# Five row buffers for the gathered expert rows, and another timetable for the dot products around the change of phase

## The chip, the core and the metric

One NeuronCore of a Trainium2 chip runs one program. Its engines are TensorE (PE), VectorE (DVE), ScalarE (ACT), GpSimd (POOL) and SyncE (SP), which issues most of the DMAs; POOL issues the gathers. Each engine works through its own instructions in the order in which they stand in the program, and waits on semaphores where it needs another engine's or a DMA's result. The metric is the time of one execution on the device in microseconds (us), lower is better: the median of three executions.

## The reference

One layer of a hybrid block on 512 tokens of width 1024, in float32. The part that matters here is the second half, a product-key retrieval (PEER) over 128 x 128 = 16384 experts, of which each is one row of `expert_u` and one of `expert_v`:

```python
q = (xb @ w_q).reshape(p, PEER_HEADS, 2, PEER_DK_HALF)
sc = jnp.einsum('phcd,hcnd->phcn', q, sub_keys)
top_s, top_i = lax.top_k(sc, PEER_TOPK)                    # 16 of 128 keys, twice per head
...
best_s, best_pos = lax.top_k(cand_s, PEER_TOPK)            # 16 of the 256 pairs
idx = jnp.take_along_axis(cand_i, best_pos, axis=-1)
g = jax.nn.softmax(best_s, axis=-1)
act = jax.nn.gelu(jnp.einsum('phkd,pd->phk', expert_u[idx], xb), approximate=False)
return jnp.einsum('phk,phkd->pd', g * act, expert_v[idx])  # 8 heads x 16 experts a token
```

Before it stand the adaLN projections, a mixer (gated convolution and RG-LRU) with its projections, and behind it the last residual and RMSNorm.

## The kernel before

**The two ways to the experts.** For 384 of the 512 tokens (tiles 1 to 3) the kernel doesn't gather: it multiplies the tokens with *all* experts and masks with gates. For tile 0, and for the u side of the first 64 tokens of tile 1, it gathers expert rows by index. So the activation phase (u phase) has 128 chunks of 128 experts, and each needs 24 matmuls of 320 columns on PE (`u_chunk`, whose `mm3` splits each product into three of reduced precision: lines 90 to 92), and the value phase (v phase) has 128 chunks of 18 matmuls of 512 columns (`v_chunk`, line 996). Of the 128 u chunks, 124 (`CE`) run in the u phase's loop at line 930, and the last four stand between the first v chunks (list `jobs`).

**What each chunk needs.** SP loads 512 KB of weights (`wraw`, line 71, four buffers, issued up to five chunks ahead and only when a buffer is free). ACT rounds them (`whi`, line 76), DVE makes the rest (`wlo`, line 81, two chunks ahead of PE). In the u phase ACT evicts each chunk's PSUM tile with a GELU (`act`, line 817), and part of the activations is spilled to DRAM (`Ad`). In the v phase every pair of chunks needs the gates (loaded from `Gd` in bursts: lines 847 and 860), `cf` (ACT line 880, DVE line 882), `ch` (ACT line 886) and `cl` (DVE line 893).

**The sparse work.** `dots()` has 192 steps, one for each gathered column of rows: a gather on POOL (`gath`, line 729: 128 rows of 4 KB into a `rows` buffer) and a dot product on DVE (`scr`, line 750). `sums()` has 128 steps: a gather from `v` and a multiply-add on DVE (`ys`, line 766). `ahead()` says how many rows are fetched ahead: the buffer count less one in the u phase, six in the v phase. In the u phase there are `GB_E` = 4 `rows` buffers; late in it three more (`rows2`) come from a pool of the v phase.

**What sets the order.** All of this is one schedule written out by Python. In the u phase, `turn(k)` chooses after each chunk whose generator takes the next step on DVE (searches `s`, remaining searches `r`, gates `g`, dots `d`), as long as the planner's DVE account (`dve[0]`, with 1320 for a dot) is behind its PE account (`pe[0]`, 3530 a chunk). In the v phase a fixed share of the sparse steps follows each chunk (line 1037). At chunk `KD` = 118 the u phase's search and gate work is flushed and its memory is handed to the v phase's pools. `topk_tile` is the search that turns scores into the 16 best experts of a tile, with small SBUF tiles of its own (`cand`, `oh`, `pf`, `bf`, `g`).

In the text chunk k is the u chunk k of the loop at line 930, and v chunk n the n-th chunk of the v phase. On DVE `wlo` of chunk k + 2 stands where the loop is at chunk k.

Of the kernel before, what the change touches and what calls it, by code (L numbers as in the profile page):

```python
# [8 lines left out]
F32 = mybir.dt.float32  # L9
FR = mybir.dt.float32r  # L10
F16 = mybir.dt.float16
# [3 lines left out]
OP = mybir.AluOpType  # L15
# [3 lines left out]
D = 1024  # L19
KB = 8  # L20
NT = 4
NE = 128
# [12 lines left out]
def block_kernel(ctx, tc, xT, small, w_ada1, w_ada, b_ada, w_in, w_r, w_i, w_out, w_q, keys, uT, u, v, final_g, out):  # L35
    nc = tc.nc
# [282 lines left out]
    for cb in range(4):  # L319
# [23 lines left out]
        a = mt("a")  # L343
# [5 lines left out]
        h = mt("h")  # L349
# [67 lines left out]
    sel = ctx.enter_context(tc.tile_pool(name="sel", bufs=1, side="right"))  # L417
# [24 lines left out]
    scp = ep.enter_context(tc.tile_pool(name="scp", bufs=1, side="right"))  # L442
# [63 lines left out]
    topk = ep.enter_context(tc.tile_pool(name="topk", bufs=1))  # L506
# [1 line left out]
    psE = psx.enter_context(tc.tile_pool(name="psE", bufs=1, space=PS))  # L508

    st16 = topk.tile([128, 16], F16, name="st16")  # L510
    s16a = topk.tile([128, 16], F32, name="s16a")
    s16b = topk.tile([128, 16], F32, name="s16b")
    nc.vector.tensor_scalar(s16a, iota[:, :16], 8.0, 8.0, op0=OP.mult, op1=OP.add)
    nc.vector.scalar_tensor_tensor(s16a, iota[:, :16], 16.0, s16a, op0=OP.mult, op1=OP.min)
    nc.vector.tensor_scalar(s16b, iota[:, :16], 4.0, 24.0, op0=OP.mult, op1=OP.add)
# [3 lines left out]
    io16 = topk.tile([128, 16], F16, name="io16")  # L519
# [6 lines left out]
    selB = sel.tile([128, 3, XB], F32, name="selB")  # L526

    def topk_tile(t):
        cand = topk.tile([128, 8, 64], F32, name="cand")
        for a, na, nb, o in ((0, 1, 16, 0), (1, 3, 8, 16), (4, 4, 4, 40), (8, 8, 1, 56)):  # L530
            shc = [128, 8, na, nb]
            nc.vector.tensor_tensor(cand[:, :, o:o + na * nb].rearrange("p h (a b) -> p h a b", b=nb),
# [19 lines left out]
        nc.vector.tensor_tensor(msk, pos, msk, op=OP.bitwise_and)  # L552
        pf = topk.tile([128, 8, 16], F16, name="pf")
        nc.vector.tensor_copy(pf, pos)
        bf = topk.tile([128, 8, 16], F16, name="bf")
        nc.vector.tensor_copy(bf, msk)
        yield 1450
        shp = [128, 8, 16, 16]
        ij = topk.tile([128, 2, 8, 16], F32, name="ij")
        for w in range(2):  # L560
            oh = topk.tile(shp, F16, name="oh")
            yield None
            key, ref, cmp, src = ((pf, st16, OP.is_ge, dif), (bf, io16, OP.is_equal, tif[:, :, 1, :]))[w]
            nc.scalar.activation(oh, key[:, :, :, None].to_broadcast(shp), AF.Copy)
            ac[0] += 1930
            if w == 0:
                nc.scalar.activation(g, g, AF.Exp)
            yield None
            nc.vector.tensor_tensor(oh, oh, ref[:, None, None, :].to_broadcast(shp), op=cmp)
            nc.vector.tensor_tensor(oh, oh, src[:, :, None, :].to_broadcast(shp), op=OP.mult)  # L570
            yield 2300
            for n in (8, 4, 2):
                nc.vector.tensor_add(oh[:, :, :, 0:n], oh[:, :, :, 0:n], oh[:, :, :, n:2 * n])
            nc.vector.tensor_add(ij[:, w], oh[:, :, :, 0], oh[:, :, :, 1])
            yield 1400
# [111 lines left out]
    def gates_E():  # L687
        for t in range(1, NT):
            while gready.get(t, NE) > cur[0]:
                yield None  # L690
            yield from gates_tile(t, range(4 if t == 1 else 0, 8), selT[t])
        while len(bdone) < XB:
            yield None
        yield None
        for e in range(2):
            es = slice(XB * e, XB * (e + 1))
            nc.scalar.activation(act_p[es, es], act_b[es, :], AF.Gelu)
        pt = psE.tile([128, 4, 128], F32, name="ps_t")
        nc.tensor.matmul(pt[:, 0, 0:XB], act_p, sel2, start=True, stop=True)
        yield None  # L700
        nc.vector.tensor_mul(selB[:, 2, :], pt[:, 0, 0:XB], selB[:, 2, :])
        yield from gates_tile(1, range(4), selB, 0)
        while gpre or gpost or stores:
            gates_step(None)
            yield None

    acts = sel.tile([128, 128], F32, name="acts")
    act_b = sel.tile([128, XB], F32, name="act_b")
    act_p = sel.tile([128, 2 * XB], F32, name="act_p")
    nc.vector.memset(act_p, 0.0)  # L710
    bdone = []

    rows = {}
    late = []
    taken = [0]

    def row_tile():
        taken[0] += 1
        if late and taken[0] > late[1] and taken[0] % 7 in (1, 3, 5):
            return late[0].tile([128, D], F32, name="rows2", bufs=3)  # L720
        return rowp.tile([128, D], F32, name="rows", bufs=GB_E)

    def ahead():
# [181 lines left out]
    def turn(k):  # L905

        awake = [g for g in "gsrd" if g in gens and asleep[g] <= k]
        if gopen and "g" in gens:
            gt = 96 * (k + 1 - gopen[0]) / (KD - KG - gopen[0])
            if "g" in awake and given["g"] < gt and ac[0] < pe[0] + AD:  # L910
                return "g"
            if "s" in awake and (given["g"] < gt and ac[0] < pe[0] + AD or given["s"] < NS * (k - gopen[0]) / (KD - gopen[0])):
                return "s"
        elif "s" in awake:
            return "s"
        elif "r" in awake and ("d" not in awake or given["d"] >= DS * (k - first[0])):
            return "r"
        for g in "dsg" if ac[0] < pe[0] + AD else "ds":
            if g in awake:
                return g  # L920
# [92 lines left out]
    for k in range(CE, len(jobs)):  # L1013
# [20 lines left out]
            pe[0] += 4090  # L1034
            dve[0] += 2005
        if kind == "v":
            share = min((n + 1) / (NE - VE), 1) * (steps + 0.31 * (NE - RB)) - 0.31 * max(n + 1 - RB, 0)
            while done < share and next(sparse, None):
                done += 1
    fin = vp.tile([128, 2, 3, D], F32, name="gt", bufs=1)  # L1040
# [40 lines left out]
XB = 64  # L1081
# [9 lines left out]
DS = 1.0  # L1091
XD = 1
CE = 124
GB_E = 4
RB = 32
ZL = 1
XE = 5
# [52 lines left out]
```

## Time and profile before

| | |
|---|---|
| Median of three executions | 1411.56 us (1410.68 to 1412.37) |
| The profiled execution | 1409.24 us |
| Its span from the first instruction to the last | 1407.5 us |
| PE / DVE / ACT / POOL busy | 96% / 87% / 52% / 38% of the span |
| First u chunk on PE | 310 us from the span's start |
| Last matmul of the u phase's loop | 839.5 us |
| Last matmul | 1393 us |
| DMA | 440.10 MB, mean 313 GB/s |

Times in views of the trace are us from the span's start. An engine's busy time is the union of its instructions' times; PE's instructions overlap each other, so that its busy share says little, and the distance from one matmul's start to the next is what counts. In a row of the timeline stand start, duration, engine, line, operation, what is written and read; in square brackets the idle time of the engine before it, and who ended it. A `DMA share` of about 1 says that all 16 DMA engines were occupied.

### The profile page before, as it was taken

What the parts mean: (1) busy time and instruction counts of PE and PEld (TensorE: products, weight loads), DVE (VectorE), ACT (ScalarE), POOL (GpSimd) and SP (SyncE); (2) the same over time, 40 slices, a digit from 0 to 9 for tenths busy, and PEclk for the clock granted to TensorE, in tenths of its full rate; (3) what the DMA queues carried; (4) which work ended last, traced back from release to release, by engine and by line L of the source; (5) the groups of instructions that cost most, each with busy time, mean ns of one, the idle gap of its engine ahead of it and who ended that gap; (6) DMA issues with size and microseconds to landing.
All of it is one profiled execution on the core that took longest, in us unless ns stands there. A gap on an engine that the chain in (4) does not pass through costs nothing.

```text
span 1407.5 us, 22023 instructions
## 1 busy us (share of the span) xinstructions
PE 1357.2 (96%) x7739; PEld 1176.0 (84%) x7739; DVE 1231.5 (87%) x2470; ACT 735.2 (52%) x1212; POOL 540.1 (38%) x334
## 2 busy tenths in 40 slices
PE   5999998999999999999999989999999999999996
PEld 2566777779999999999999988877778888878884
DVE  6676565799999999989999967989989898999998
ACT  3554433536489699956996533333333333343342
POOL 0000000000135434514333335666757676766770
PEclk9999999999999999999999999999999999999998
DMA  9575323124689899978999899999999999999994
GB/s 378 213 256 197 132 85 103 53 91 138 206 273 406 320 346 367 391 251 309 353 369 373 301 402 383 368 359 413 410 413 414 415 412 415 414 407 413 414 369 177
DMA packets 146931, 440.10 MB, mean 313 GB/s; under 512 B 14722, under 2 KB 42370, under 8 KB 144772
## 3 DMA queue, kind: packets, MB, share of 16 engines
q1 hardware_dynamic: 99812, 267.75, 51.4%
q0 software_dynamic: 46720, 169.89, 31.5%
q8 instruction: 61, 1.00, 0.3%
q10 hardware_dynamic: 288, 1.05, 0.2%
q14 instruction: 50, 0.41, 0.1%
HBM read 393.54 MB, written 45.09 MB: 312 GB/s over the span
## 4 chain that ended last, share of the span: by engine, by line
PE 32%; issue 24%; DMA 20%; DVE 16%; POOL 6%; ACT 1%; DVEq 0%; POOLq 0%; SPq 0%; ACTq 0%
DMA wraw<-in_v_dram 13%; PE acc L996 7%; POOL rows L729 6%; PE ps_z L90 5%; PE ps_z L92 5%; PE ps_z L91 5%; DMA rows<-in_u_dram,idx_s 3%; DVE wlo L81 3%; DVE scr L750 3%; DVE ys L766 3%; DMA rows<-in_u_dram,idx_b 2%; PE ps_act L90 2%; DVE cf L882 2%; PE ps_act L91 2%; PE ps_act L92 2%
## 5 line engine op out<-in xcount | busy, mean ns | idle before, releaser
L76 ACT ACTIVATE whi<-wraw 128x1024 fp32r<-128x1024 f32 x292 | 308.4, 1057 | 392.9 <-DMA wraw<-in_v_dram 170.0
L81 DVE TENSOR_TENSOR wlo<-wraw,whi 128x1024 fp32r<-128x1024 f32 x292 | 356.1, 1221 | 82.5 <-ACT whi L76 81.3
L90 PE MATMUL ps_act<-h,whi 128*128 128x320 f32 x1024 | 322.4, 315 | 1.5 <-ACT sc L494 1.2
L91 PE MATMUL ps_act<-h,whi 128*128 128x320 f32 x1024 | 317.0, 310 | 0.0
L92 PE MATMUL ps_act<-h,wlo 128*128 128x320 f32 x1024 | 316.8, 309 | 0.0
L729 POOL DMA_INDIRECT rows<-in_u_dram,idx_s x128 | 201.1, 1571 | 226.5 <-DVE scr L750 187.3
L729 POOL DMA_INDIRECT rows<-in_v_dram,idx_s x128 | 234.7, 1833 | 108.9 <-DVE ys L766 82.1
L996 PE MATMUL acc<-whi,cl 128*128 128x512 f32 x750 | 232.7, 392 | 6.1 <-DVE cl L893 6.1
L996 PE MATMUL acc<-whi,ch 128*128 128x512 f32 x750 | 232.8, 391 | 5.2 <-ACT act L817 3.9
L996 PE MATMUL acc<-wlo,ch 128*128 128x512 f32 x750 | 232.0, 390 | 0.0
L90 PEld LDWEIGHTS ps_act<-h,whi 128*128 128x128 f32 x1024 | 193.0, 189 | 2.1 <-ACT sc L494 1.4
L91 PEld LDWEIGHTS ps_act<-h,whi 128*128 128x128 f32 x1024 | 193.0, 189 | 0.2
L92 PEld LDWEIGHTS ps_act<-h,wlo 128*128 128x128 f32 x1024 | 192.7, 188 | 0.0
L729 POOL DMA_INDIRECT rows<-in_u_dram,idx_b x64 | 99.2, 1550 | 211.7 <-DVE scr L750 105.6
L996 PEld LDWEIGHTS acc<-whi,cl 128*128 128x128 f32 x750 | 140.5, 189 | 38.8 <-DVE cl L893 10.2
L996 PEld LDWEIGHTS acc<-whi,ch 128*128 128x128 f32 x750 | 141.0, 188 | 35.7 <-ACT act L817 4.7
L996 PEld LDWEIGHTS acc<-wlo,ch 128*128 128x128 f32 x750 | 141.4, 189 | 29.7
L766 DVE SCALAR_TENSOR_TENSOR ys<-rows,acts,ys 128x1024 f32<-128x1024 f32 x127 | 162.8, 1282 | 1.6
L750 DVE SCALAR_TENSOR_TENSOR scr<-rows,h2n 128x1024 f16<-128x1024 f32 x128 | 156.4, 1222 | 8.2 <-DMA rows<-in_u_dram,idx_s 6.7
L406 POOL DMA_DIRECT2D x1d<-xn x8 | 4.6, 569 | 282.5 <-DVE wlo L81 234.9
L817 ACT ACTIVATE act<-ps_act 128x320 f32<-128x320 f32 x128 | 55.4, 433 | 102.3 <-PE ps_act L92 100.4
L621 PE MATMUL ps_gt<-igh,jh 128*128 128x128 f32 x768 | 97.4, 275 | 2.6 <-DVE igh L615 0.9
(258 smaller groups left out, 1888.4 us busy)
## 6 DMA issues: line engine op xcount, KB each, us to landing
wraw<-in_uT_dram SPq DMA_DIRECT2D x128, 512.0 KB, 6.8
wraw<-in_v_dram SPq DMA_DIRECT2D x128, 512.0 KB, 10.1
Gd<-stg SPq DMA_DIRECT2D x46, 512.0 KB, 7.0
wada<-in_w_ada_dram SPq DMA_DIRECT2D x16, 1024.0 KB, 5.3
Ad<-act SPq DMA_DIRECT2D x48, 320.0 KB, 7.7
act<-Ad SPq DMA_DIRECT2D x48, 320.0 KB, 11.4
h<-Gd SPq DMA_DIRECT2D x12, 1024.0 KB, 17.7
wraw<-in_w_in_dram SPq DMA_DIRECT2D x20, 512.0 KB, 6.0
```

The costliest lines, as they stand in the source:

```text
L76: nc.scalar.activation(hi, raw, AF.Copy)
L81: nc.vector.tensor_sub(lo, raw, hi.bitcast(F32))
L90: nc.tensor.matmul(ps, hi[:, k, :], xh(k), start=first and k == ks[0], stop=False)
L91: nc.tensor.matmul(ps, hi[:, k, :], xl(k), start=False, stop=False)
L92: nc.tensor.matmul(ps, lo[:, k, :], xh(k), start=False, stop=last and k == ks[-1])
L621: nc.tensor.matmul(pg[:, :, k], jh[:, k, :], ig[:, k, :], start=True, stop=True)
L729: nc.gpsimd.indirect_dma_start(out=r[:, :], out_offset=None, in_=table, in_offset=bass.IndirectOffsetOnAxis(ap=idxs[:, k:k + 1], axis=0))
L750: nc.vector.scalar_tensor_tensor(scr, rows.pop(n), 1.0, hn, op0=OP.mult, op1=OP.mult, accum_out=dst[:, k:k + 1])
L766: nc.vector.scalar_tensor_tensor(ys, rows.pop(k), acts[:, k:k + 1], ys, op0=OP.mult, op1=OP.add)
L817: nc.scalar.activation(act[c // 2][:, c % 2], ps, AF.Gelu)
L882: nc.vector.tensor_mul(cf[:, :, XB:].rearrange("p c (g t) -> p c g t", t=16), act.pop(vorder[2 * q] // 2).rearrange("p c (g t) -> p c g t" ...
L996: nc.tensor.matmul(accs[b][e], st[:, bs], mv[:, e * 512:(e + 1) * 512], start=first, stop=last)
```

## The change

**Memory, and with it a fifth row buffer.** Some small tiles lose their own memory: `cand` now lies in the `oh` buffer, the second key (`bf`) takes the `pf` buffer after the first has been read, `act_p` takes the `g` buffer, and the two constants `s16a` and `s16b` two `rep` buffers. `GB_E` goes from 4 to 5, so that the u phase fetches four rows ahead; of the late `rows2` there are two in place of three, so that the v phase still has seven.

**The dots' timetable.** `turn` leaves the dots out of the choice when more than `DR` = 1.15 dots a chunk were given so far, from chunk `CE - QU` = 118 on, and when the chunk has had one (even chunks) or two (odd chunks); before, a chunk's dots were limited (to `XD` = 1) only once the gates' generator had ended. In the v phase the sparse steps begin `QV` = 3 chunks later, and the line of line 1037 is steeper so that it ends where it did.

```diff
-    s16a = topk.tile([128, 16], F32, name="s16a")
-    s16b = topk.tile([128, 16], F32, name="s16b")
+    s16a, s16b = (scp.tile([128, 128], F32, name="rep", bufs=2)[:, 0:16] for _ in range(2))
...
-        cand = topk.tile([128, 8, 64], F32, name="cand")
+        cand = topk.tile([128, 8, 16, 16], F16, name="oh").rearrange("p h a b -> p (h a b)").bitcast(F32)
+        cand = cand[:, 0:512].rearrange("p (h c) -> p h c", h=8)
...
-        bf = topk.tile([128, 8, 16], F16, name="bf")
-        nc.vector.tensor_copy(bf, msk)
-        yield 1450
+        yield 1350
...
             oh = topk.tile(shp, F16, name="oh")
+            if w == 1:
+                pf = topk.tile([128, 8, 16], F16, name="pf")
+                nc.vector.tensor_copy(pf, msk)
             yield None
-            key, ref, cmp, src = ((pf, st16, OP.is_ge, dif), (bf, io16, OP.is_equal, tif[:, :, 1, :]))[w]
+            key, ref, cmp, src = ((pf, st16, OP.is_ge, dif), (pf, io16, OP.is_equal, tif[:, :, 1, :]))[w]
...
+        act_p = topk.tile([128, 8, 16], F32, name="g").rearrange("p a b -> p (a b)")
+        nc.vector.memset(act_p, 0.0)
         for e in range(2):
...
-    act_p = sel.tile([128, 2 * XB], F32, name="act_p")
-    nc.vector.memset(act_p, 0.0)
...
-        if late and taken[0] > late[1] and taken[0] % 7 in (1, 3, 5):
-            return late[0].tile([128, D], F32, name="rows2", bufs=3)
+        if late and taken[0] > late[1] and taken[0] % 7 in (2, 5):
+            return late[0].tile([128, D], F32, name="rows2", bufs=2)
...
         awake = [g for g in "gsrd" if g in gens and asleep[g] <= k]
+        if "d" in awake and (given["d"] >= DR * (k + 1 - first[0]) or k >= CE - QU or xd > k % 2):
+            awake.remove("d")
...
-            share = min((n + 1) / (NE - VE), 1) * (steps + 0.31 * (NE - RB)) - 0.31 * max(n + 1 - RB, 0)
+            share = min(max(n + 1 - QV, 0) / (NE - VE - QV), 1) * (steps + 0.31 * (NE - RB)) - 0.31 * max(n + 1 - RB, 0)
...
-GB_E = 4
+GB_E = 5
+DR = 1.15
+QU = 6
+QV = 3
```

**What moves on DVE at the change of phase.** This is DVE's order in the kernel before, from the `wlo` that stands at loop chunk 117 to the first `cf` of the v phase; each L750 row is a dot product.

```order
L81 TENSOR_TENSOR wlo<-wraw,whi 128x1024
L750 SCALAR_TENSOR_TENSOR scr,acts<-rows,h2n 128x1024
L81 TENSOR_TENSOR wlo<-wraw,whi 128x1024 x2
L750 SCALAR_TENSOR_TENSOR scr,acts<-rows,h2n 128x1024
L81 TENSOR_TENSOR wlo<-wraw,whi 128x1024
L750 SCALAR_TENSOR_TENSOR scr,acts<-rows,h2n 128x1024
L81 TENSOR_TENSOR wlo<-wraw,whi 128x1024
L750 SCALAR_TENSOR_TENSOR scr,acts<-rows,h2n 128x1024
L81 TENSOR_TENSOR wlo<-wraw,whi 128x1024
L750 SCALAR_TENSOR_TENSOR scr,acts<-rows,h2n 128x1024
L882 TENSOR_TENSOR cf<-act,gt 128x2x320
```

The same place in the changed kernel, where a dot product has line 751 and `cf` and `cl` have lines 883 and 894; it goes on to the first dots of the v phase.

```order
L81 TENSOR_TENSOR wlo<-wraw,whi 128x1024
L751 SCALAR_TENSOR_TENSOR scr,acts<-rows,h2n 128x1024
L81 TENSOR_TENSOR wlo<-wraw,whi 128x1024 x5
L883 TENSOR_TENSOR cf<-act,gt 128x2x320
L81 TENSOR_TENSOR wlo<-wraw,whi 128x1024
L894 TENSOR_TENSOR cl<-cf,ch 128x768
L81 TENSOR_TENSOR wlo<-wraw,whi 128x1024
L883 TENSOR_TENSOR cf<-act,gt 128x2x320
L81 TENSOR_TENSOR wlo<-wraw,whi 128x1024 x2
L894 TENSOR_TENSOR cl<-cf,ch 128x768
L81 TENSOR_TENSOR wlo<-wraw,whi 128x1024 x2
L883 TENSOR_TENSOR cf<-act,gt 128x2x320
```

The dots after loop chunk 117 are gone from here, and with them the gathers that their buffers would have released on POOL; the next dot stands behind v chunk 3. Counted through the whole order: up to chunk 117 both kernels have 111 of the 192 dots; in chunks 118 to 123 the kernel before has 5 and the changed one none; behind them stand 76 before and 81 now.

**What moves on DVE in the v phase.** The kernel before at v chunks 12 and 13, with the `cf` of one pair of chunks and its `cl`:

```order
L81 TENSOR_TENSOR wlo<-wraw,whi 128x1024
L882 TENSOR_TENSOR cf<-act,gt 128x2x320
L750 SCALAR_TENSOR_TENSOR scr,acts<-rows,h2n 128x1024
L81 TENSOR_TENSOR wlo<-wraw,whi 128x1024
L893 TENSOR_TENSOR cl<-cf,ch 128x768
L750 SCALAR_TENSOR_TENSOR scr,acts<-rows_10028,h2n 128x1024
L750 SCALAR_TENSOR_TENSOR scr,acts<-rows,h2n 128x1024
```

The changed kernel at the same two chunks (`rows_10012` is a buffer of the `rows2` pool):

```order
L81 TENSOR_TENSOR wlo<-wraw,whi 128x1024
L883 TENSOR_TENSOR cf<-act,gt 128x2x320
L751 SCALAR_TENSOR_TENSOR scr,acts<-rows,h2n 128x1024
L751 SCALAR_TENSOR_TENSOR scr,acts<-rows_10012,h2n 128x1024
L81 TENSOR_TENSOR wlo<-wraw,whi 128x1024
L894 TENSOR_TENSOR cl<-cf,ch 128x768
L751 SCALAR_TENSOR_TENSOR scr,acts<-rows,h2n 128x1024 x2
```

Where the kernel before now and then has one dot a chunk, the changed one has two nearly throughout. By the line of line 1037, with 76 + 128 = 204 and 81 + 128 = 209 steps, a chunk had (204 + 29.76) / 127 = 1.84 steps up to v chunk 31 and 0.31 fewer behind it, 1.53; now it has none in three chunks, then (209 + 29.76) / 124 = 1.93, and behind v chunk 31 1.62.

## Prediction

> **What bounds the kernel now.** I read the page's busy shares and slices first, then busy time by stretches, then the waits of PE, then the timeline around each wait.
>
> ```profile
> PE 1357.2 (96%) x7739; PEld 1176.0 (84%) x7739; DVE 1231.5 (87%) x2470; ACT 735.2 (52%) x1212; POOL 540.1 (38%) x334
> DVE  6676565799999999989999967989989898999998
> ```
>
> PE's 96% says little, since its matmuls overlap; the slices say that from the eighth on DVE is nearly as full as PE. So the question is who waits for whom. These are the waits of PE in four stretches: the u phase (320 to 839 us), the change of phase (839 to 880), the first v chunks with dots (880 to 1048), and the rest of the v phase (1048 to 1382).
>
> ```profile
> PE ps_gt L621 <- DVE igh L615: 0.9, 2, 0.6
> PE acc L996 <- ACT act L817: 3.9, 2, 3.5
> PE acc L996 <- DVE cl L893: 5.3, 7, 2.2
> PE acc L996 <- ACT ch L886: 1.3, 2, 0.9
> PE acc L996 <- DVE cl L893: 0.8, 1, 0.8
> ```
>
> The first row, the longest of the u phase, is under a microsecond in 519: PE paces the u phase. At the change of phase PE waits 3.9 us in two waits, in the first dot-laden v chunks 6.6 us, and in the last 334 us once. All that a new timetable can win lies in these places.
>
> The largest is the change of phase. PE's last u matmul, its first two v matmuls, and the first matmul behind the first v chunk:
>
> ```profile
> 839.45 0.31 PE L92 MATMUL ps_act<-h,wlo 128*128 128x320 f32 x1
> 843.22 0.80 PE L996 MATMUL acc<-whi,ch 128*128 128x512 f32 x1 [3.46 <-ACT act L817]
> 844.49 0.80 PE L996 MATMUL acc<-whi,ch 128*128 128x512 f32 x1 [0.48 <-ACT act L817]
> 850.60 0.31 PE L90 MATMUL ps_act<-h,whi 128*128 128x320 f32 x1
> 842.00:849.00 7.00, 5.30 (x12) 3.87 (x13) 6.96 (x9) 2.44 (x4) 2.09 (x2) 0.51 1.06 340
> 1100.00:1200.00 100.00, 100.00 (x442) 82.68 (x442) 94.10 (x88) 40.23 (x51) 68.15 (x37) 1.00 1.03 414
> ```
>
> The last two rows are stretches; their columns are the stretch, its length, busy time (and instructions) of PE, PE's weight loads, DVE, ACT and POOL, the granted clock, DMA share and GB/s. An undisturbed v chunk costs 18 x 100/442 = 4.07 us. From 839.60 (one u step of 0.15 behind the last) to 850.60 pass 11.0 us: **6.9 us are lost here**, 3.6 before the first matmul and 3.3 after it, about one of those at the second wait and the rest because PE's clock stood at 0.51 after the gap.
>
> Why PE waits there is on ACT, DVE and SP:
>
> ```profile
> 840.71 1.06 ACT L76 ACTIVATE whi<-wraw 128x1024 fp32r<-128x1024 f32 x1 [7.52 <-DMA wraw<-in_uT_dram]
> 842.75 0.42 ACT L817 ACTIVATE act<-ps_act 128x320 f32<-128x320 f32 x1
> 844.02 0.42 ACT L817 ACTIVATE act<-ps_act 128x320 f32<-128x320 f32 x1
> 838.62 0.82 DVE L882 TENSOR_TENSOR cf<-act,gt 128x640 f32<-128x640 f32 x1 [4.90 <-DMA gt<-Gd]
> 823.22 6.81 SPq L860 DMA_DIRECT2D gt<-Gd  x3
> 830.08 3.70 SPq L71 DMA_DIRECT2D wraw<-in_uT_dram  x1
> ```
>
> ACT is in order, and the rounding of u chunk 124's weights holds up everything behind it for 7.5 us: the `ch` of v chunk 0 and the two evictions. Those weights were issued only at 830, behind three gate loads that took SP 6.8 us to issue, and landed 10.6 us later. The DMA engines were full (this stretch, with POOL's column showing who shares them):
>
> ```profile
> 800.00:830.00 30.00, 30.00 (x211) 30.00 (x210) 24.68 (x36) 12.29 (x18) 16.60 (x12) 1.00 1.03 408
> 830.00:870.00 40.00, 36.07 (x196) 32.52 (x195) 25.86 (x32) 14.89 (x21) 15.30 (x12) 0.91 1.02 380
> ```
>
> POOL's 12 instructions are gathers of 128 x 4 KB = 0.524 MB: 6.3 of the 12.2 MB of 800 to 830.
>
> **The change part by part.** *The empty chunks around the change of phase.* Five dots and their gathers leave chunks 118 to 123, and none come back before v chunk 3 (some 862 us by the old clock). From about 820 to 862 the gathers, half of the traffic above, are gone. Then the gates land several microseconds before 838, and the weights issued at 830 or sooner take less than their 10.6 us. Late next is the eviction of the last u chunk, which can't start before that chunk's matmuls end (839.76) and takes 0.42 us, so the second v matmul starts near 840.3 in place of 839.8. I leave 0.6 us of the 6.9, and no halved clock behind so short a gap. **Term: -6.3 us**, bounds -6.9 (nothing left) and 0 (below, the rival in which SP is the cause).
>
> *First v chunks.* These rows are DVE's dots and weight splits from 930 to 1003, and the stretch itself:
>
> ```profile
> L750 DVE SCALAR_TENSOR_TENSOR scr<-rows,h2n 128x1024 f16<-128x1024 f32 x32 | 39.1, 1222 | 0.5
> 930.00:1003.00 73.00, 69.93 (x301) 55.60 (x300) 69.49 (x97) 25.51 (x33) 52.07 (x31) 1.00 1.02 400
> ```
>
> DVE works 69.5 of 73 us, so here it sets the pace, and PE waits for `cl`. From v chunk 17 to 31 the new line has 1.93 - 1.84 = 0.09 more dots a chunk: 15 x 0.09 x 1.22 = 1.6 us, and none of it is covered. The three chunks without dots don't help, because `wlo` can't run further ahead than its buffers. **Term: +1.6 us** (bounds 0, if the lead that DVE brings from there covers it, and 4: all 31 - 3 chunks at that rate, 3.1, and a longer wait at the first load of gates).
>
> *Rest of the v phase.* DVE's three large groups from 1048 to 1382, the waits of ACT for weights in the v phase, and PE's wait behind such a late load (the first, in the stretch above):
>
> ```profile
> L766 DVE SCALAR_TENSOR_TENSOR ys<-rows,acts,ys 128x1024 f32<-128x1024 f32 x126 | 161.5, 1282 | 1.6
> L81 DVE TENSOR_TENSOR wlo<-wraw,whi 128x1024 fp32r<-128x1024 f32 x83 | 101.2, 1220 | 16.6 <-ACT whi L76 16.6
> ACT whi L76 <- DMA wraw<-in_v_dram: 169.4, 63, 8.0
> 929.19 0.74 PE L996 MATMUL acc<-whi,cl 128*128 128x512 f32 x2 [2.17 <-DVE cl L893]
> ```
>
> DVE is idle 16.6 + 1.6 = 18.2 us here, nearly all waiting for weights. The new line adds 1.62 - 1.53 = 0.09 steps in each of 81 chunks: 7.3 x 1.28 = 9.3 us of DVE work, half of that idle time. On average it fits; but the idle time comes when loads are late, once in 16 chunks with the gates, and then DVE's work is not ahead as far as it was: 16 x 0.09 x 1.28 = 1.8 us a burst. PE has room there except where it waits already, which is at two of the five bursts behind chunk 31 (one in the row of 5.3 us, one the 0.8). I charge these two with 0.8 each. **Term: +1.6 us** (bounds 0 and 5 x 1.8 = 9.2).
>
> *The u phase.* The number of dots up to chunk 117 is the same (111); they are only spread more evenly, and a fifth buffer fetches a row more ahead. DVE's waits for rows late in the u phase, from 800 to 842:
>
> ```profile
> DVE scr L750 <- DMA rows<-in_u_dram,idx_s: 4.8, 5, 1.5
> ```
>
> These 4.8 us go, and cost PE nothing before (no wait of PE names DVE there beyond the 0.9 above). Sharing buffers costs no new wait of weight: `cand`, `oh` and `pf` are written and read in turn by DVE in order, and ACT's copy into `oh` waited for DVE's `pf` before as well. If DVE's work comes too late for a gate matmul, PE waits as in that 0.9 row. **Term: 0**, bounds -0.9 (that wait gone) and +1.8 (twice as much on top). The moved constants and the later `memset` are under 1 us of DVE work each beside chunks that PE paces: nothing.
>
> *Sum.* -6.3 + 1.6 + 1.6 + 0 = -3.1 us. The profiled execution took 1409.24 us (span 1407.5 and 1.7 around it), so it becomes 1406.1; the median of the runs lies 2.3 us above that execution, and the forecast for the median is 1411.56 - 3.1 = **1408.5 us**.
>
> **The rivals.** *Nothing is given back.* The added DVE work hides: for it, the one wait of PE after 1048; against it, the DVE-paced stretch before. Then 1411.56 - 6.3 = 1405.3 us.
>
> *The stall stays, because SP and not the gathers makes it.* SP took 6.8 us to issue three gate loads, and the weights behind them came late for that reason; if issuing is what takes the time, taking gathers away moves little. [...] Against it, two rows of the same trace, a larger gate load later on, and its size:
>
> ```profile
> 892.51 0.44 SPq L847 DMA_DIRECT2D h<-Gd  x1
> h<-Gd SPq DMA_DIRECT2D x12, 1024.0 KB, 17.7
> gt<-Gd SPq DMA_DIRECT2D x6, 512.0 KB, 10.2
> ```
>
> A load of 1024 KB is issued in 0.44 us, three of 512 KB in 6.8: so SP was held up by full engines, and this rival is the less likely. It gives 1411.56 + 3.2 = 1414.8 us, or less with half of the stall gone.
>
> *The DMA engines become the bound of the v phase, and it ends slower.* The place is v chunk 3 to about 110. Before that point the old kernel had already issued gathers that the new one has still to issue: ten between 843 and 869 (the 12 of the row 830 to 870, less two before 843), and four in balance before 843 (76 + 128 steps less three rows ahead, against 81 + 128 less four). That is 14 x 0.524 = 7.3 MB, and at 412 GB/s, which the trace reaches (row 1100 to 1200: 414), 17.8 us. Old stretches with room take some of it:
>
> ```profile
> 870.00:900.00 30.00, 30.00 (x142) 25.41 (x142) 27.81 (x41) 11.83 (x17) 19.52 (x12) 1.00 0.96 358
> 900.00:1000.00 100.00, 94.77 (x410) 75.88 (x409) 89.63 (x123) 35.80 (x46) 65.58 (x41) 1.00 1.01 394
> ```
>
> 54 x 30 + 18 x 100 GB/s us = 3.4 MB, 8.3 us. The rest, 9.5 us, would be PE's wait: 1411.56 - 6.3 + 9.5 = 1414.8 us. It decides from the point where rows are read as soon as they land; before, `ys` waited 1.6 us in 126 times, so rows come early, and the lead can shrink instead. [...] The page's slices of GB/s never show more than 415:
>
> ```profile
> GB/s 378 213 256 197 132 85 103 53 91 138 206 273 406 320 346 367 391 251 309 353 369 373 301 402 383 368 359 413 410 413 414 415 412 415 414 407 413 414 369 177
> ```
>
> So I keep the 412.
>
> **How the numbers follow.** The forecast (with its own range 1406 to 1411) has 0.45, nothing given back 0.25, the stall that stays 0.12, DMA as the bound 0.13, anything else 0.05. About 0.2%, 2.8 us, is what a measurement of this kernel can tell from no change. Faster than 1408.7 are the second case and half of the first, 0.48; slower than 1414.4 the last two in part and most of the rest, 0.17; between them 0.35. The range leaves out a tenth on each side: below, a clean gain of more than 7; above, the bounds of the v terms: 1404 to 1415.
>
> **What would show it.** Right: the gap between the last u matmul and the first v matmul under 1 us, clock 1.00 there, no POOL gather from some 820 us to v chunk 3, PE's waits for `cl` from v chunk 17 to 31 longer by one to two us, waits after 1048 two or three in place of one. Wrong: a gap above 2 us with SP still several us in the gate loads (the second rival), or DVE waiting for `rows` in the v phase (the third), or PE waits of several us before chunk 118 for gates.

## The result, and the profile after

| | before | after |
|---|---|---|
| Median of six executions | 1410.74 us (1408.89 to 1412.37) | 1420.61 us (1418.6 to 1423.04) |
| The profiled execution, its span | 1409.24, 1407.5 us | 1418.6, 1416.8 us |

The changed kernel is slower: the ratio is 1.0074, with a 95% interval from 1.0063 to 1.0085. The forecast was 1408.5 us and its range ended at 1415.

From the page of the changed kernel, the busy shares, DVE's slices and the slices of GB/s (a slice is 35.4 us):

```profile
PE 1357.7 (96%) x7739; PEld 1175.0 (83%) x7739; DVE 1233.2 (87%) x2472; ACT 733.5 (52%) x1208; POOL 518.1 (37%) x334
DVE  6676555899999999899999947799999899899998
GB/s 378 208 267 193 121 89 97 60 83 149 219 304 391 293 355 370 339 254 344 373 365 349 386 352 219 408 377 415 411 416 412 414 412 413 407 415 411 399 382 171
```

The busy shares are those of before. What stands out are two slices. The 25th, from 850 to 885 us, moved 219 GB/s where the kernel before moved 383; the one ahead of it 352 where that moved 402. Over the same stretch DVE drops to 4 and 7 tenths.

**The change of phase** went as the prediction said. PE's last u matmul, its first two v matmuls and the first matmul behind the first v chunk stand in the timeline of PE; the weights of u chunk 124 in that of ACT; the gate loads in that of SP:

```profile
839.15 0.31 PE L92 MATMUL ps_act<-h,wlo 128*128 128x320 f32 x1
839.29 0.40 PE L999 MATMUL acc<-whi,ch 128*128 128x512 f32 x1
839.98 0.50 PE L999 MATMUL acc<-whi,ch 128*128 128x512 f32 x1 [0.29 <-ACT act L818]
834.61 1.06 ACT L76 ACTIVATE whi<-wraw 128x1024 fp32r<-128x1024 f32 x1 [1.72 <-DMA wraw<-in_uT_dram]
818.20 9.07 SPq L861 DMA_DIRECT2D gt<-Gd  x3
```

The v phase begins directly behind the u phase, and the matmul behind the first v chunk starts at 843.97. By the prediction's own measure (from the last u matmul on, less 0.15 and 4.07 us) 0.60 us are lost here, where the kernel before lost 6.93: **6.3 us gained**, exactly the term. SP still takes 9.07 us in the gate loads; from 818 to 828 us the DMA share was 1.05, at 399 GB/s.

**Where the time came from instead.** The last u matmul stands 0.3 us earlier than before and 6.3 us were gained behind it, but the span is 9.3 us longer. So the rest of the program lost 9.3 + 6.3 + 0.3 = 15.9 us. PE's waits in the changed kernel, first from 880 to 1048 us, then from 1048 to 1395:

```profile
PE acc L999 <- ACT ch L887: 5.8, 2, 3.7
PE acc L999 <- DVE cl L894: 2.7, 4, 1.4
PE acc L999 <- DVE cl L894: 3.8, 5, 2.4
PE acc L999 <- ACT ch L887: 2.3, 2, 1.7
PE acc L992 <- DVE cl L894: 1.6, 1, 1.6
```

They are 8.5 us in place of 6.6, and 7.7 in place of 0.8: 8.8 us more. In the first stretch it is the waits that name `ch` that grew, from 1.3 to 5.8; those for `cl` fell from 5.3 to 2.7. And three times the granted clock fell, in stretches of 4 us (columns as in the prediction, the clock third from the end):

```profile
915.00:919.00 4.00, 4.00 (x11) 3.10 (x12) 3.37 (x6) 0.09 (x1) 1.59 (x1) 0.58 1.06 407
980.00:984.00 4.00, 4.00 (x11) 2.93 (x11) 3.93 (x7) 1.06 (x1) 2.04 (x2) 0.57 1.03 419
1110.00:1114.00 4.00, 4.00 (x13) 3.12 (x12) 3.96 (x5) 2.10 (x3) 2.17 (x2) 0.57 1.03 418
```

I estimate the cost of each from its clock, 4 x 0.43 = 1.7 us, so 5.1 together. Waits and clock make 13.9 of the 15.9 us; where the other two go isn't shown.

**What PE waits for.** The longest wait, in ACT's and PE's timeline:

```profile
912.81 1.06 ACT L76 ACTIVATE whi<-wraw 128x1024 fp32r<-128x1024 f32 x1 [12.62 <-DMA wraw<-in_v_dram]
914.99 0.73 PE L999 MATMUL acc<-whi,ch 128*128 128x512 f32 x2 [3.66 <-ACT ch L887]
```

PE names ACT, and ACT had waited 12.6 us for a load of weights, with `ch` queued behind it. Over the later v phase (1048 to 1395) ACT's waits for weights are, before and after:

```profile
ACT whi L76 <- DMA wraw<-in_v_dram: 102.4, 41, 8.0
```

```profile
ACT whi L76 <- DMA wraw<-in_v_dram: 126.2, 50, 7.7
```

DVE, on which the prediction priced this phase, is not fuller. These are its groups from 1048 to 1382 us, and its only wait for rows from 880 on:

```profile
L767 DVE SCALAR_TENSOR_TENSOR ys<-rows,acts,ys 128x1024 f32<-128x1024 f32 x122 | 156.3, 1281 | 1.6
L81 DVE TENSOR_TENSOR wlo<-wraw,whi 128x1024 fp32r<-128x1024 f32 x80 | 97.6, 1221 | 18.6 <-ACT whi L76 18.6
DVE scr L751 <- DMA rows<-in_u_dram,idx_s: 0.4, 1, 0.4
```

It sits idle 1.6 + 18.6 us, as it did before (1.6 + 16.6). What was given up is DMA time. The stretches of the changed kernel:

```profile
820.00:862.00 42.00, 41.71 (x255) 39.21 (x254) 18.80 (x18) 17.47 (x25) 0.00 (x0) 1.00 0.82 284
862.00:880.00 18.00, 18.00 (x92) 15.62 (x91) 15.89 (x23) 7.20 (x10) 9.64 (x6) 1.00 0.72 245
880.00:1000.00 120.00, 112.31 (x475) 90.41 (x474) 108.44 (x151) 40.99 (x53) 80.34 (x51) 0.97 1.01 397
1000.00:1100.00 100.00, 99.16 (x438) 81.80 (x437) 92.28 (x113) 35.72 (x46) 62.70 (x39) 1.00 1.04 413
```

and of the kernel before:

```profile
820.00:862.00 42.00, 38.07 (x221) 35.30 (x220) 29.30 (x37) 14.29 (x22) 15.35 (x12) 0.92 1.03 384
862.00:880.00 18.00, 18.00 (x98) 16.06 (x97) 13.81 (x19) 8.15 (x12) 9.90 (x7) 1.00 0.99 392
880.00:1000.00 120.00, 114.77 (x498) 92.45 (x497) 109.49 (x152) 43.35 (x56) 80.57 (x49) 1.00 1.00 385
1000.00:1100.00 100.00, 98.64 (x434) 81.03 (x433) 91.57 (x105) 35.87 (x47) 64.13 (x39) 1.00 1.03 412
```

From 820 to 880 the changed kernel moves 284 x 42 + 245 x 18 = 16.3 MB, the kernel before 23.2: 6.85 MB are left for later, 16.6 us at 412 GB/s. The bytes are the same in all (440.10 MB), and from 1000 us on both kernels run at 412 to 413 with the DMA share above 1, although the changed one has 5.4 MB more waiting: there is nothing to catch up with. Only 880 to 1000 took something, (397 - 385) x 120 = 1.4 MB or 3.5 us. POOL shows what is missing:

```profile
816.06 0.94 POOL L730 DMA_INDIRECT rows<-in_u_dram,idx_s  x1 [3.10 <-DVE scr L751]
864.01 1.80 POOL L730 DMA_INDIRECT rows<-in_u_dram,idx_s  x1 [47.01 <-DVE scr L751]
```

No gather starts for 48 us, because all five buffers are full and the next dot that frees one stands behind v chunk 3. At 864 the first one goes; 6 gathers start from 820 to 880, where the kernel before has 19.

### The profile page after: what moved, and what is told of

Its sections match the earlier page's. It is cut to its first block, busy times and chain, and to the rows that moved or that the text cites. A ratio compares the mean times of both kernels' runs of the same rounds, so it can differ in the third digit from the quotient of the medians.

```text
span 1416.8 us, 22009 instructions
## 1 busy us (share of the span) xinstructions
PE 1357.7 (96%) x7739; PEld 1175.0 (83%) x7739; DVE 1233.2 (87%) x2472; ACT 733.5 (52%) x1208; POOL 518.1 (37%) x334
## 2 busy tenths in 40 slices
DMA packets 146931, 440.10 MB, mean 311 GB/s; under 512 B 14722, under 2 KB 42370, under 8 KB 144772
## 3 DMA queue, kind: packets, MB, share of 16 engines
q10 hardware_dynamic: 288, 1.05, 0.2%
## 4 chain that ended last, share of the span: by engine, by line
issue 26%; DVE 26%; PE 24%; DMA 15%; POOL 6%; ACT 2%; DVEq 0%; POOLq 0%; SPq 0%; ACTq 0%
DMA wraw<-in_v_dram 12%; POOL rows L730 6%; DVE wlo L81 5%; PE ps_z L90 4%; PE ps_z L92 4%; PE ps_z L91 4%; DVE ys L767 4%; DVE scr L751 3%; DVE cf L883 2%; DVE cl L894 2%; PE acc L999 2%; PE ps_act L90 2%; PE ps_act L92 2%; PE ps_act L91 2%; PE ps_gt L622 2%
## 5 line engine op out<-in xcount | busy, mean ns | idle before, releaser
L730 POOL DMA_INDIRECT rows<-in_v_dram,idx_s x128 | 218.8, 1709 | 113.2 <-DVE ys L767 90.3
L730 POOL DMA_INDIRECT rows<-in_u_dram,idx_b x64 | 91.9, 1436 | 249.9 <-DVE scr L751 128.0
```

Of the source, the lines that this page charges most:

```text
L730: nc.gpsimd.indirect_dma_start(out=r[:, :], out_offset=None, in_=table, in_offset=bass.IndirectOffsetOnAxis(ap=idxs[:, k:k + 1], axis=0))
```

## The experiments

Three theories were put against each other. **A**: the gathers left out of the emptied chunks come back where the DMA engines are full. **B**: the fifth buffer, the split of the late buffers and the shared tiles cost it. **C**: DVE has more steps a chunk in the v phase. All runs stand beside executions of the kernel before on the same chip (medians 1409.5 to 1410.2). "Lost" is the change of phase measured as above, "MB" what the DMA moved from 820 to 880 us, and "gathers" how many started there. "Behind" is the rest of the profiled execution, from the first matmul behind the first v chunk to the end of the span; "lost" and "behind" are of one execution each, the median is of several.

| Kernel | gathers | MB | lost, us | behind, us | median, us | ratio to before |
|---|---|---|---|---|---|---|
| before | 19 | 23.2 | 6.9 | 556.9 | 1410.7 | |
| after | 6 | 16.3 | 0.6 | 572.8 | 1420.6 | 1.0074 [1.0063, 1.0085] |
| e1 both stretches filled | 18 | 20.9 | 1.6 | 560.7 | 1404.8 | 0.9967 [0.9957, 0.9978] |
| e2 emptied stretches alone | 8 | 17.6 | 1.8 | 578.4 | 1424.1 | 1.0094 [1.0077, 1.0111] |
| e3 14 gathers left out | 6 | 16.5 | 0.6 | 563.6 | 1410.2 | 1.0008 [0.9998, 1.0018] |
| e4 14 dots made short | 6 | 16.6 | 0.6 | 573.4 | 1419.7 | 1.0068 [1.0051, 1.0085] |
| e5 end of the u phase empty | 13 | 19.3 | 0.6 | 568.2 | 1412.8 | 1.0022 [1.0013, 1.0031] |
| e6 start of the v phase empty | 11 | 18.4 | 2.7 | 570.4 | 1417.0 | 1.0048 [1.0035, 1.0062] |
| e7 five buffers alone | 17 | 22.2 | 7.6 | 555.8 | 1408.5 | 0.9987 [0.9975, 1.0] |
| e8 even dots alone | 19 | 22.4 | 4.3 | 557.8 | 1404.6 | 0.9962 [0.9948, 0.9975] |
| e9 gathers early | 8 | 17.1 | 0.6 | 569.7 | 1417.0 | 1.0052 [1.0037, 1.0067] |
| e10 seven buffers at once | 16 | 21.7 | 6.9 | 557.7 | 1409.7 | 1.0004 [0.9992, 1.0015] |
| e11 gate loads apart | 17 | 22.0 | 4.4 | 554.3 | 1405.5 | 0.9969 [0.9958, 0.998] |
| e12 v dots sooner | 20 | 23.2 | 2.6 | 557.1 | 1405.7 | 0.9972 [0.9963, 0.9982] |

### Which part does the harm: e1 and e2

e1 is the changed kernel with both stretches filled again; e2 is the kernel before with nothing but the two stretches.

```diff
-QU = 6
-QV = 3
+QU = 0
+QV = 0
```

> The changed kernel without the two edits that empty the chunks around the change of phase (the cut-off from chunk 118 on and the three v chunks without sparse steps): five buffers, shared tiles and the even spread of the dots stay, and the dots stand in the same numbers as in the kernel before (111 up to chunk 117, 5 in chunks 118 to 123, 6 in the first three v chunks). Theory A (DMA: the gathers that leave the emptied chunks come back where the DMA engines are full) gives the time of the kernel before, 1409 to 1412 us, with PE's wait of some 4 us back at the change of phase. Theory B (the fifth buffer with its 5 + 2 split, or the shared tiles, cost the time) gives 1417 to 1421.

```diff
         awake = [g for g in "gsrd" if g in gens and asleep[g] <= k]
+        if "d" in awake and k >= CE - QU:
+            awake.remove("d")
...
-            share = min((n + 1) / (NE - VE), 1) * (steps + 0.31 * (NE - RB)) - 0.31 * max(n + 1 - RB, 0)
+            share = min(max(n + 1 - QV, 0) / (NE - VE - QV), 1) * (steps + 0.31 * (NE - RB)) - 0.31 * max(n + 1 - RB, 0)
```

> The kernel before, four buffers, with those two edits alone. Theory A gives 1418 to 1422 us, theory B 1404 to 1411. Both expect PE's wait at the change of phase to be under 1 us.

e1 took 1404.8 us, 15.8 less than the changed kernel and less than the kernel before; e2 took 1424.1. So the emptied stretches do the harm, and without the rest of the change they do no less (1424.1 lies above A's range too, but the intervals of e2 and of the changed kernel overlap); theory B falls. e1 came out below what A expected too, because the wait at the change of phase hardly returned. In e1, PE's wait there and the stretches:

```profile
PE acc L999 <- ACT act L818: 1.3, 1, 1.3
820.00:862.00 42.00, 40.73 (x248) 38.18 (x247) 26.06 (x33) 15.16 (x22) 11.38 (x9) 1.00 0.95 339
862.00:880.00 18.00, 18.00 (x94) 15.77 (x93) 17.86 (x26) 8.31 (x12) 13.93 (x10) 1.00 0.98 371
```

It loses 1.6 us there although the dots stay in chunks 118 to 123. This loss isn't the same in each execution: e6, e11 and e12, whose program is that of e1 up to this place, lose 2.7, 4.4 and 2.6 in theirs. Emptying the chunks bought one to four microseconds on top of that, and cost all the rest.

### Gathers or dots: e3 and e4

In e3 fourteen of the gathers behind the emptied stretch are left out (those dots read `h2n` in their place); in e4 the gathers stay and the same fourteen dots cover 64 of 1024 columns.

```diff
+        if table is u and key in SKIP:
+            rows.setdefault(key, h2n)
...
+SKIP = range(131, 187, 4)
```

> The changed kernel without the gathers of 14 of its 128 u rows for tile 0, every fourth from row column 67 on (v chunks 14 to 44); their dot products stay and read another tile instead, so that 14 columns of these activations are not the reference's. DVE's work is the same. Theory A: 14 x 0.524 MB at 412 GB/s are 17.8 us of DMA time less, and most of what the change lost comes back: 1405 to 1411 us. Theory C (DVE: more sparse steps a chunk are what PE waits for) expects 1418 to 1421.

```diff
-            nc.vector.scalar_tensor_tensor(scr, rows.pop(n), 1.0, hn, op0=OP.mult, op1=OP.mult,
+            w = 64 if n in SKIP else D
+            nc.vector.scalar_tensor_tensor(scr[:, 0:w], rows.pop(n)[:, 0:w], 1.0, hn[:, 0:w], op0=OP.mult, op1=OP.mult,
...
+SKIP = range(131, 187, 4)
```

> The changed kernel with the gathers of those same 14 columns, but their dot products over 64 of the 1024 columns of a row, so that these 14 columns of activations are not the reference's. DMA's work is the same, DVE's is 14 x 1.1 = 15 us less. Theory C expects 1405 to 1412 us, theory A 1417 to 1421.

Without the gathers the time falls by 10.4 us; with the dots cut short, by 0.9, which lies within the spread of the changed kernel's executions, though DVE is busy for 14.9 us less from 880 to 1380 us (449.0 in place of 464.0). Theory C falls. The 10.4 us are 0.74 a gather, less than its 0.524 MB at 412 GB/s (1.27 us). My guess, which no run tests, is that the debt was paid off slowly, since only one dot in four lost its gather; the first long wait, at 912 us, stayed (3.9 us; 3.7 in the changed kernel).

### Which of the two stretches: e5 and e6

The changed kernel with `QV = 0` (e5) and with `QU = 0` (e6).

> The changed kernel with QV = 0: the chunks 118 to 123 stay without dots, the first v chunks get theirs back (dots up to chunk 117, in 118 to 123, in v chunks 0 to 2, in 3 to 15, in 16 to 31, later: 111, 0, 6, 25, 30, 20). Beside the kernel with both stretches filled (1404.8) five dots and their gathers are moved out, beside the changed kernel (1420.6) six are moved back. If every moved gather costs its share of the 15.8 us between those two (1.4 us each): 1411 to 1413, with DMA at 820 to 862 below 320 GB/s and at 862 to 880 above 340. If the v chunks' gap alone does the harm: 1404 to 1406. If the gap at the end of the u phase alone does it: 1419 to 1421.

> The changed kernel with QU = 0: dots in chunks 118 to 123 stay, the v phase begins with three chunks without (111, 5, 0, 25, 30, 21). Six dots and their gathers are moved out. By 1.4 us each: 1412 to 1415, with DMA at 862 to 880 below 300 GB/s. If the gap at the end of the u phase alone does the harm: 1404 to 1406; if that of the v chunks alone: 1419 to 1421. In all cases the wait at the change of phase should be about that of the kernel with both filled (1.3 us), not of the kernel before (6.9).

1412.8 and 1417.0 us: 8.0 and 12.2 above e1, so both stretches cost. Together they cost 15.8, less than the sum. The 1.4 us a dot of the expectation held for the five of e5 (1.6) and was low for the six of e6 (2.0). The stretch from 862 to 880 us, first in e5, then in e6:

```profile
862.00:880.00 18.00, 18.00 (x89) 15.49 (x89) 15.89 (x22) 7.94 (x11) 10.51 (x7) 1.00 0.77 267
```

```profile
862.00:880.00 18.00, 18.00 (x96) 15.92 (x95) 15.58 (x21) 6.24 (x9) 8.21 (x6) 1.00 0.66 227
```

For e5 the expectation was wrong here (above 340), and from 820 to 862 us too (344 GB/s, below 320 expected). The late buffers count from the tenth gather behind chunk 118 on, so with five dots fewer the fill-up to seven buffers, at 868 to 877 us in e1, comes at 879 to 886: the missing dots leave the next stretch emptier too.

### What makes e1 faster than the kernel before: e7 and e8

e7 is the changed kernel without its timetable (`QU = 0`, `QV = 0`, and the two lines in `turn` left out); e8 is the kernel before with the rule on the number of dots and nothing else:

```diff
         awake = [g for g in "gsrd" if g in gens and asleep[g] <= k]
+        if "d" in awake and (given["d"] >= DR * (k + 1 - first[0]) or xd > k % 2):
+            awake.remove("d")
...
 GB_E = 4
+DR = 1.15
```

> The changed kernel without any of the new timetable (QU = 0, QV = 0, and the line in turn that drops the dots left out): five row buffers and the shared tiles alone, dots 112, 5, 6, 24, 29, 16. If the fifth buffer makes the gain of the kernel with both stretches filled (it lets a gather start before the burst of weight and gate loads): 1404 to 1406, and a wait of 1 to 2 us at the change of phase. If spreading the dots (DR and the limit a chunk) makes it: 1409 to 1411 as before, and about 7 us lost at the change of phase.

> The kernel before with the line in turn that holds the dots to DR = 1.15 a chunk and to one or two in a chunk, and with nothing else: four row buffers, no stretch without dots (112, 5, 6, 24, 29, 16). The mirror of the run before: if spreading makes the gain, 1404 to 1406 with the wait at the change of phase at 1 to 2 us; if the fifth buffer makes it, 1409 to 1411 with about 7 us lost there. If it needs both, both runs stay at 1408 to 1411.

(The numbers of dots in the expectation of e8 are those of e7; e8 has 111, 5, 6, 24, 29, 17.) Five buffers alone give 1408.5 us, and the loss at the change of phase stays, 7.6 us. The rule alone gives 1404.6, with four buffers, and the loss goes down to 4.3, not to the 1 to 2 us of the expectation. The profiled execution of e8 is 3.4 us shorter than that of the kernel before: 2.7 less is lost at the change of phase, the last u matmul stands 1.7 earlier, and behind there are 0.9 more. What the rule moves is small: the kernel before and e7 have 12 dots in chunks 110 to 117, e8 and e1 have 10. It shows in the arrival of u chunk 124's weights, ACT's rows of e7, e1 and e10 (below):

```profile
841.04 1.06 ACT L76 ACTIVATE whi<-wraw 128x1024 fp32r<-128x1024 f32 x1 [8.21 <-DMA wraw<-in_uT_dram]
```

```profile
836.41 1.06 ACT L76 ACTIVATE whi<-wraw 128x1024 fp32r<-128x1024 f32 x1 [3.53 <-DMA wraw<-in_uT_dram]
```

```profile
841.45 1.06 ACT L76 ACTIVATE whi<-wraw 128x1024 fp32r<-128x1024 f32 x1 [7.81 <-DMA wraw<-in_uT_dram]
```

From 799 to 838 us the kernel before, e7 and e10 start 13 gathers each, and the weights come at 840.7, 841.0 and 841.5; e1, e2, e6, e8, e11 and e12 start 9 to 11, and they come between 836.1 and 838.7; the changed kernel starts 7, and they come at 834.6. The losses go with them: 6.9 to 7.6 us, 1.6 to 4.4, and 0.6. So the stall goes with the last few gathers ahead of the change of phase. With two to four of the thirteen away, between two fifths (e11) and five sixths (e1) of the 6.3 us are gained that taking six away gains.

### Moving gathers alone: e9 and e10

In both the two late buffers count from chunk 118 on; e9 is otherwise the changed kernel and issues a gather after each of four chunks, e10 is e1. DVE's order is kept.

```diff
-            late[:] = [gp, taken[0] + 10]
+            late[:] = [gp, taken[0]]
+        if KD < k < KD + 5:
+            pre = len(bdone) + k - KD + 2
+            gath(u, usteps[pre][0], usteps[pre][3], pre)
```

> The changed kernel, in which only gathers are moved: the two late row buffers count from chunk 118 on, and one gather each is issued in chunks 119 to 122, so that five rows and not three lie ready when the dots begin again behind v chunk 3, and the fill-up to seven buffers at 893 us falls into the empty stretch. DVE's order, with its stretch of nine chunks without dots, stays. If the DMA engines' work left out of that stretch is what costs (15.8 us for the twelve gathers that the kernel with both stretches filled has issued more by 880 us), four gathers earlier are worth 3 to 5 us: 1415 to 1418, with more than 284 GB/s at 820 to 862. If the dots' place on DVE costs: 1419 to 1422. If it is only the burst of gathers at 893 beside the gate loads: the wait of 3.66 us at 915 is gone and the time falls by 4, with the later waits for cl and ch unchanged.

> The kernel with QU = 0 and QV = 0 (1404.8), with the two late row buffers counted from chunk 118 on in place of ten gathers later, so that the two gathers of the fill-up come at 820 to 850 us (339 GB/s there, about 3 MB of room) and not at 868 to 877. If DMA work done before 880 us is worth its time at 412 GB/s: 2 gathers, 1.05 MB, up to 2.5 us less, 1402 to 1404. If that stretch is too close to the change of phase and its gate loads: the wait there (1.3 us) grows by as much, 1404 to 1406.

e9 took 1417.0 us, 3.6 less than the changed kernel and within A's range, but not as meant. Only one gather came early:

```profile
824.98 1.04 POOL L730 DMA_INDIRECT rows<-in_u_dram,idx_s  x1 [7.31 <-DMA Ad<-act]
864.68 1.80 POOL L730 DMA_INDIRECT rows<-in_u_dram,idx_s  x1 [38.66 <-DVE scr L751]
```

POOL runs ahead of the other engines until a buffer is missing (38.66 us of waiting for DVE's `scr` in its row), so the changed kernel's gathers already stood in all five buffers; of the four, one had the late buffer, and the next waited for a dot again. By 880 us e9 has two gathers more than the changed kernel, and the burst at 893 is gone, so it doesn't tell apart whether the bytes or the burst cost; its first long waits after 880 are 2.1 and 2.3 us and not 3.7. e10 is the clean one: the same dots as e1, two gathers more from 799 to 838 us, and the loss at the change of phase goes to 6.9 us (1.6 to 4.4 in the four runs with e1's beginning), the time from 1404.8 to 1409.7. SP issues the weights of u chunk 124 at 828.3 us in e1 and at 828.2 in e10, and ACT begins to round them at 836.4 and at 841.5. Gathers and not dots make that stall, nor does SP's order. Behind the change of phase e10 takes 3.0 us less than e1 (557.7 and 560.7), at it 5.3 more: moving DMA work earlier costs more than it gains where it meets the weights that the change of phase waits for. No run has the gathers in the emptied stretch without the dots; that their bytes are what costs rests on e3, e4 and the order of the table.

### The rest: e11 and e12

e11 is e1 with its first three gate loads at v chunks 6, 8 and 10; e12 is e1 with `QV = -2`.

```diff
-            m = n + (4 - t if n < 16 else 13 - 3 * t)
+            m = n + (7 - 2 * t if n < 16 else 13 - 3 * t)
```

> The kernel with QU = 0 and QV = 0 (1404.8), with its three first gate loads of 1 MB at v chunks 6, 8 and 10 in place of 8, 9 and 10. The bytes and their stretch are the same, only their burst is flatter. If the burst makes the waits at 912 and 923 us (3.9 us together): 1402 to 1404. If the DMA engines are simply full from 880 us on, nothing is gained: 1404 to 1406.

> The other direction: the changed kernel with QU = 0 and QV = -2, so that the v phase begins with two chunks' worth of dots more instead of three chunks without (dots 111, 5, 10, 23, 29, 14; with QV = 0 they are 111, 5, 6, 24, 29, 17). Six dots follow each other behind v chunk 0. If DMA work done before 880 us is worth its time, the four dots' gathers come some microseconds sooner into a stretch with room (339 GB/s at 820 to 862, 371 at 862 to 880, of 412) and the time falls below that of the kernel with both stretches filled (1404.8): 1400 to 1403. If the six dots in a row hold up DVE's wlo and cl there, PE waits for them between 845 and 870 and the time is 1405 to 1409.

Neither gained: 1405.5 and 1405.7 us. In e11 the waits at 912 and 923 us went (no wait of PE for `ch` or `cl` is longer than 1.5 us), and 4.4 us were lost at the change of phase in place of 1.6, ahead of anything that this edit moves. Behind it the profiled execution of e11 takes 6.4 us less than that of e1, but the medians show no gain, so what the burst of gate loads is worth stays open. In e12 DMA moved 23.2 MB from 820 to 880 us, as much as before, and two microseconds of it came back as a wait for `wlo` behind the six dots in a row:

```profile
853.83 0.31 PE L91 MATMUL ps_act<-h,whi 128*128 128x320 f32 x1
856.16 0.42 PE L92 MATMUL ps_act<-h,wlo 128*128 128x320 f32 x1 [2.02 <-DVE wlo L81]
```

The best versions stay e8 and e1, which can't be told apart: 0.4% and 0.3% faster than the kernel before.

## Why the prediction was wrong

**Change of phase, -6.3 us: right.** 6.93 became 0.60 us, by the reason given: without the gathers the weights of chunk 124 land early (834.6), and late next is the last eviction. The granted clock stood at 1.00 from 820 to 862 us, as the term had it (0.92 before). Of the sign named for the rival in which SP makes the stall, one half, SP still several us in the gate loads, is there (9.07 us), and the other, a gap above 2 us, is not (0.29): SP's time in the gate loads is not what makes the stall. e10 shows it from the other side: it brings the stall back (6.9 us) by gathers alone, with the weights issued at the same time as in e1 (828.2 and 828.3 us).

**u phase, 0: right.** The last u matmul stands 0.3 us earlier.

**First v chunks, +1.6, and the rest of the v phase, +1.6: the step that failed.** They charged the moved dots to DVE: "0.09 more dots a chunk" times 1.22 us, and a late gate load twice. The waits of the first stretch did grow by 1.9 us, which looks like a hit, but the waits for DVE's `cl`, which the term is about, fell by 2.6, and those for `ch`, behind late weights, grew by 4.5; and e4 shows that DVE's work has no part in the loss (0.9 us for 14 dots). Each dot carried a gather, and the price of moving it is the gather's place in the DMA's work. The terms, 3.2 us together, should have been one: 6.85 MB not moved from 820 to 880 us, 16.6 us at 412 GB/s, against 15.9 that were lost behind the change of phase.

**The rival with the DMA engines as the bound had the mechanism, and a wrong credit.** It counted 14 gathers, 7.3 MB (measured 6.85), 17.8 us, and then took off 8.3 us, since "Old stretches with room take some of it", namely 870 to 900 and 900 to 1000. But a gather starts when a dot has freed a buffer (the one at 864.01 had waited 47.01 us for that), and the same change had moved those dots: the next stretch with room got emptier with it (245 GB/s from 862 to 880, where there had been 392), and 880 to 1000 took 3.5 us. Without the credit the rival says 1411.56 - 6.3 + 17.8 = 1423.1 us; with the 3.5 us that were taken, 1419.6, and 1420.6 was measured. It also got 0.13 where the row of 407 to 415 GB/s in the page's last third, which stood in the prediction, should have made it the likeliest: a phase that already moved 412 GB/s took nothing more of what an earlier one had left (413 from 1000 to 1100 us).

**Its sign was wrong too.** "DVE waiting for `rows` in the v phase" didn't happen (0.4 us). What was late is the weights (12.6 us in ACT's row), and PE names `ch` or `cl`. The likely reason, which no run tests, is that rows are fetched six ahead, while a chunk's weights are loaded into four buffers that come free late.

**The ceiling.** The rival was priced at 412 GB/s, a rate of the trace, and that rate held: with 5.4 MB more waiting, the stretch 1000 to 1100 moved 413 GB/s in place of 412. The most that a stretch of 100 us showed was 414, as in the kernel before from 1100 to 1200. The measured rate is the bound here.

**Nothing is given back** would have needed the DMA to have room in the v phase, where it moved 413 GB/s in place of 412; e1 and e8 do reach that rival's 1405.3 us, but by taking two or three gathers away ahead of the change of phase, and not by emptying two stretches.

## What to carry to other kernels

When work is moved that brings a transfer with it, make two sums, one of engine time and one of bytes, and look at the GB/s of the stretch that takes them in: where it moves no more with more waiting (here 413 GB/s in place of 412), count bytes left undone ahead of it as time (here 15.9 us for 6.85 MB). Count a stretch with room as room only if the transfers can start there (here 245 GB/s from 862 to 880 us, where there had been 392), so ask what frees their buffers. And to shorten a stall made by contention, move the few transfers that meet it, and look whether a spread takes enough of them away before emptying the whole stretch (here 1.6 to 4.4 us lost with 9 to 11 gathers ahead of it, 6.9 to 7.6 with 13).

## What was not expected of the hardware

How much of the put-off DMA work comes back can be read only roughly, from the columns "MB" and "behind". e1 moves 2.3 MB less than the kernel before (5.5 us at 412 GB/s) and takes 3.8 us more behind; the changed kernel moves 4.6 MB less than e1 (11.1 us) and takes 12.1 more, of which 1.7 can be clock, by the estimate above: from 1100 to 1200 us the granted clock was 0.98 in the changed kernel and 1.00 in e1, from 880 to 1000 it was 0.97 in both. Of the first megabyte and a half nothing is seen to come back: the six kernels with 21.7 to 23.2 MB take 554.3 to 557.8 us, in no order. And bytes aren't all: e2 moves 1.3 MB more than the changed kernel and takes 5.6 us more behind. In it PE stands still for 8.9 us at once, at 912 us, behind a load of weights for which ACT waits 13.8 us; why it comes so late there no run shows.

Some waits of two to four microseconds cost more than themselves, by the clock, in the v phase as at the change of phase (0.51 from 842 to 849 us, behind 3.46 us, in the kernel before). Behind the changed kernel's wait of 3.66 us the granted clock was 0.58 over 4 us, and the other two of its stretches near 0.57 stand behind waits of 2.14 us (at 979 us) and 2.39 us (at 1109 us). In e5 it fell to 0.70 over 3.5 us behind a wait of 2.83 us; in e6, behind 2.32 us, it didn't. The wait of 2.14 us in the changed kernel and that of 2.32 us in e6, and the stretches at those of e5 and e6:

```profile
979.25 0.73 PE L999 MATMUL acc<-whi,ch 128*128 128x512 f32 x2 [2.14 <-ACT ch L887]
```

```profile
980.97 0.73 PE L999 MATMUL acc<-whi,ch 128*128 128x512 f32 x2 [2.32 <-ACT ch L887]
```

```profile
913.50:917.00 3.50, 3.50 (x11) 2.58 (x12) 3.27 (x6) 0.00 (x0) 1.20 (x1) 0.70 1.04 423
```

```profile
980.00:984.00 4.00, 3.03 (x13) 2.31 (x14) 3.96 (x5) 1.56 (x3) 0.62 (x1) 1.00 1.03 421
```

So the length of the wait alone doesn't decide it: 2.14 us stood ahead of a clock of 0.57, 2.32 us ahead of one of 1.00. What does, no run shows.
